# A gated MLP on one core: two plain hidden tiles in place of three, the norm's row left out of eight tiles and applied to their product sums later, sums split at full width

## The chip, the cores and the metric

The kernel runs on one core of a Trainium2 chip. The metric is device time in microseconds (us). The kernel before took 1174.26, 1174.37 and 1175.05 us in three runs, median 1174.37. Its profiled execution is a fourth one, of 1175.14 us.

The engines of a core run their own instruction streams side by side and wait for each other by semaphores: PE (matmuls), DVE (vector), ACT (scalar), POOL and SP. In this kernel SP issues the loads, POOL the stores that add to what is in DRAM.

## The reference, cut to what matters

The network has two layers over 512 positions of width 1024. Each layer ends in a gated MLP with 2816 hidden columns; `x` is float32.

```python
def rmsnorm(x, g):
    y = x * lax.rsqrt(jnp.mean(x * x, axis=-1, keepdims=True) + EPS)
    return y * g

def conv_ffn(h, w_up, conv_w, conv_b, w_down):
    u, g = jnp.split(h @ w_up, 2, axis=-1)
    g = causal_dwconv(g, conv_w, conv_b)      # width 3 over positions
    return (jax.nn.silu(g) * u) @ w_down

x = x + conv_ffn(rmsnorm(x, norm_ffn_g[l]), ffn_w_up[l], ffn_conv_w[l], ffn_conv_b[l], ffn_w_down[l])
```

The factor of the norm is one number for each position. It must be in the gate before the convolution and the silu; the other factor `u`, and everything behind it, is linear in it.

## The kernel before

Activations lie transposed: 128 features by 512 positions in a tile, so `x` has 8 tiles and the hidden layer 22. The norm's factors, one for each position and the same in all partitions, are a tile of 128x512, the row (`norm.row`). Every operand of a matmul is split into a high part (ACT: a cast, line 143) and a low part (DVE: source minus high, line 144), and `mm3` (lines 197 to 199) makes three matmuls of a product.

`ChannelMixer` is the MLP of one layer. Its input is scaled by `gain` alone: the row is multiplied into gate and up after the projection, so that the projections of the first tile need not wait for the norm. Hidden tiles come in two ways:

- **Plain tiles** (`plain(j)`, j below `PLAIN` = 3): gate and up, 8 products each, 48 matmuls of 512 columns. Then gate times row (line 773), the convolution's three taps (one on ACT, two on DVE in line 744), silu, times row (line 778), times up (line 781), and the split into the pair `hid[j]`. The finish of the norm is woven into the first plain tile: a sum of squares, a matmul with ones, and five short operations that make the row.
- **Block steps** (`step(j)`, j from 3 to 21): gate and up of a tile together in seven block products instead of eight. Each has 4 products of 256 columns, 84 matmuls in all. Their operands are sums and differences of weight blocks (DVE, line 944) and of blocks of the activations. The latter, `block_sums` (four pairs of tiles: 4 differences of 256 columns, line 799, then 4 splits of 256 for each pair), are needed from the first step on and are woven between the projections: `EARLY` and `BEHIND_NORM` say where, and `weave` puts one behind every 16 products. `Forms` loads and prepares the weights of one step ahead, `Tail` finishes the tile of one step behind (row on the gate in line 996, on up in line 999, taps, silu, product, split).

Behind the hidden tiles come the down products: `LOADS` lists pieces of the down weights, as hidden tiles k0 to k1 and output tiles j0 to j1; `UNITS` gives each step its pieces, one from step 3 on. `down_products` makes the matmuls for one output tile in a PSUM tile (`ptr`), `add` copies it to SBUF (ACT, line 825), and POOL adds it to `xspill` in DRAM (line 826), which holds `x`. The first two pieces take hidden tiles 0 and 1 for four output tiles each (24 matmuls of 512 columns), the next four tiles 2 and 3 for two output tiles (12 matmuls), the rest four hidden tiles for two output tiles (24). The last 6 hidden tiles are multiplied by the stage that follows, after `x` is read back.

In the block steps the order on PE, ACT and DVE is the order in which the code is written (`manual_schedule`); in the plain stage and on SP and POOL a scheduler sets it. All queues are worked off in order: what stands behind a waiting instruction waits too. Weight tiles of 128x1024 are loaded into three buffers (`wr`), so a load goes out when the third load before it has been split.

Of the kernel before, what the change touches and what calls it, by code (L numbers as in the profile page):

```python
# [39 lines left out]

PLAIN, LAST = 3, 6
LOADS = [(0, 2, 0, 4), (0, 2, 4, 8)]
LOADS += [(2, 4, 2 * i, 2 * i + 2) for i in range(4)]
LOADS += [(4 * g, 4 * g + 4, 2 * i, 2 * i + 2) for g in (1, 2, 3) for i in range(4)]
EARLY, BEHIND_NORM = ({4: 1, 5: 1}, {7: 1}), (1, 1)
UNITS = {3 + i: tuple((i, j) for j in range(*LOADS[i][2:])) for i in range(len(LOADS))}

H = S // 2  # L50

# [6 lines left out]
def trunk(  # L58
# [34 lines left out]
    def sb(tag, shape, dtype=F32):  # L93
        count[0] += 1
        return pool.tile(shape, dtype, tag=tag, name=f"{tag}{count[0]}", bufs=bufs[tag])
# [46 lines left out]
    def split(hi, lo, src, on_act=True, pinned=False):  # L142
        high = A.copy(hi, src) if on_act else V.tensor_copy(hi, src)  # L143
        low = V.tensor_tensor(out=lo, in0=src, in1=f(hi), op=ALU.subtract)  # L144
        if pinned:
            pin(high)
            pin(low)
# [575 lines left out]
    class ChannelMixer:  # L723
# [9 lines left out]
        def __init__(self, l, gain, beside):  # L733
            self.l, self.act, self.norm, self.gain, self.beside = l, [], Norm(), gain, beside
            self.forms = self.block_sums()
            self.w, self.fw, self.fb = ffn_w_up[l], col[f"fw{l}"], col[f"fb{l}"]
            self.hid, self.down, self.loaded = [], {}, set()


        def taps(self, j, acc, src):  # L740
# [19 lines left out]
        def plain(self, j):  # L760
            gate = project(self.w, DFF + j * P, self.act)
            up = project(self.w, j * P, self.act, "sc")
            if self.norm.row is None:
                both = pair_of(gate, up)
                weave(self.norm.finish(), both, 1)
                for _ in range(BEHIND_NORM[self.l]):
                    next(self.forms)
                og, ou = yield from both
            else:
                og = yield from gate  # L770
                ou = None
            acc, src = sb("t", [P, S]), sb("t", [P, S])
            V.tensor_tensor(out=src, in0=og, in1=self.norm.row, op=ALU.mult)
            self.last_tap(j, acc, src)
            for _ in self.taps(j, acc, src):
                pass
            A.activation(acc, acc, AF.Silu)
            V.tensor_mul(acc, acc, self.norm.row)
            if ou is None:
                ou = yield from up  # L780
            V.tensor_tensor(out=acc, in0=ou, in1=acc, op=ALU.mult)
            self.keep(acc)

        def block_sums(self):

            self.sums = []
            for k in range(KT // 2):
                b1, b2 = sb("u", [P, S]), sb("u", [P, S])
                for t, i in ((b1, k), (b2, k + KT // 2)):
                    A.activation(t, xT[i], AF.Copy, scale=self.gain[:, i : i + 1])  # L790
                forms = []
                ta, tb = sb("t", [P, S]), sb("t", [P, S])
                for o, x, y in (
                    (ta[:, :H], b1[:, H:], b1[:, :H]),
                    (ta[:, H:], b2[:, H:], ta[:, :H]),
                    (tb[:, :H], b2[:, H:], b1[:, H:]),
                    (tb[:, H:], b2[:, :H], ta[:, H:]),
                ):
                    V.tensor_tensor(out=o, in0=x, in1=y, op=ALU.subtract)
                for t in (ta, tb):  # L800
                    for h in (t[:, :H], t[:, H:]):
                        both = sb("u", [P, S], F32R)
                        split(both[:, :H], both[:, H:], h)
                        forms.append(both)
                self.sums.append(forms)
                yield

# [6 lines left out]
        def down_products(self, q, j):  # L814
            k0, k1, j0, _ = LOADS[q]
            w = self.down[q]
            o = ps("tr")
            c = slice((j - j0) * P, (j - j0 + 1) * P)
            for k in range(k0, k1):
                mm3(o, w[0][:, k - k0, c], w[1][:, k - k0, c], *self.hid[k], k == k0, k == k1 - 1)  # L820
            return j, o

        def add(self, j, o):
            t = sb(("bias", "t")[self.l], [P, S])
            A.copy(t, o)  # L825
            G.dma_start(xspill[j], t, accum_op=ALU.add)  # L826


# [19 lines left out]

        def t(self, i):

            return [(p[i - 1][:, :H], p[i - 1][:, H:]) for p in self.sums]

        def later(self):

# [22 lines left out]
        def step(self, j, w, nxt, tail):  # L877
            def then(o, *names):
                for name in names if o is not None else ():
                    getattr(o, name)()  # L880

            def sum_products(o, r, w, i):

                self.products(r, w, self.t(i))
                A.copy(o, r[:, :H])  # L885

            new = Tail(self, j)
            then(tail, "last_block", "scaled")
            w.split_fourth()
            then(tail, "scaled_up")  # L890
            r1, r2, new.r3 = ps("mm"), ps("mm"), ps("sc")
            new.up, new.u3, new.pre = sb("t", [P, S]), sb("t", [P, S]), sb("t", [P, S])
            self.products(r1, w.a11, self.b(0, 0), True)
            A.copy(new.up[:, :H], r1[:, :H])
            then(tail, "first_tap", "second_tap", "third_tap")
            self.products(r2, w.a12, self.b(1, 0), True)
            V.tensor_tensor(out=new.up[:, :H], in0=new.up[:, :H], in1=r2[:, :H], op=ALU.add)
            sum_products(new.up[:, H:], r1, w.s2, 2)
            then(tail, "silu")
            then(nxt, "sums")  # L900
            self.products(new.r3, w.s1, self.t(1), True)
            then(tail, "gated")
            then(nxt, "split_second", "sum_third")
            sum_products(new.u3[:, :H], r1, w.s3, 3)
            then(tail, "split")
            then(nxt, "split_up")
            V.tensor_tensor(out=new.pre[:, H:], in0=new.u3[:, :H], in1=new.r3[:, :H], op=ALU.add)
            w.down_products(0, 2)
            then(nxt, "split_sums", "sum_fourth")
            w.add_down(0)  # L910
            then(nxt, "split_gate")
            w.add_down(1)
            then(nxt, "split_down")
            sum_products(new.pre[:, :H], r1, w.a22, 4)
            w.down_products(2, 4)
            self.products(new.r3, w.s4, self.b(1, 1))
            w.add_down(2)
            w.add_down(3)
            return new, nxt

    class Forms:
# [63 lines left out]
    class Tail:  # L985
# [10 lines left out]
            V.tensor_mul(self.pre, self.pre, self.mixer.norm.row)  # L996

        def scaled_up(self):
            V.tensor_mul(self.up, self.up, self.mixer.norm.row)

        def first_tap(self):
            self.acc = sb("t", [P, S])
# [591 lines left out]
```

## Time and profile before

| what | value |
|---|---|
| median of three runs | 1174.37 us |
| profiled execution / its span | 1175.14 / 1173.4 us |
| granted clock of TensorE | 0.998 |
| ACT, POOL busy, share of the span | 63%, 12% |
| layer 0: plain tiles 0, 1, 2 | 273.76, 285.13, 296.01 to 306.89 us |
| layer 1: first plain tile from | 825.80 us |
| low parts of 128x1024 (line 144) | 172, mean 1138 ns |
| row on up (line 999) | 38, mean 686 ns |
| stores from line 826 | 80, layer 0 median 6.1 us to landing, layer 1 5.9 us |

Times in a row of a timeline are its start and its length in us. A matmul's row shows its whole length, which overlaps the next one: what it costs is the distance to the start of the next. The same holds for DVE, where an operation's last part overlaps the next one's start. Where a row has brackets at its end, the engine sat idle before it for so many us, and the arrow names what it waited for.

### The profile page before, as it was taken

What the parts mean: (1) busy time and instruction counts of PE and PEld (TensorE: products, weight loads), DVE (VectorE), ACT (ScalarE), POOL (GpSimd) and SP (SyncE); (2) the same over time, 40 slices, a digit from 0 to 9 for tenths busy, and PEclk for the clock granted to TensorE, in tenths of its full rate; (3) what the DMA queues carried; (4) which work ended last, traced back from release to release, by engine and by line L of the source; (5) the groups of instructions that cost most, each with busy time, mean ns of one, the idle gap of its engine ahead of it and who ended that gap; (6) DMA issues with size and microseconds to landing.
All of it is one profiled execution on the core that took longest, in us unless ns stands there. A gap on an engine that the chain in (4) does not pass through costs nothing.

```text
span 1173.4 us, 19109 instructions
## 1 busy us (share of the span) xinstructions
PE 1163.2 (99%) x7149; PEld 1035.1 (88%) x7149; DVE 983.8 (84%) x1768; ACT 744.2 (63%) x1345; POOL 143.0 (12%) x238
## 2 busy tenths in 40 slices
PE   9999999999999999999999999999999999999997
PEld 9988888888899999999888888778789999999986
DVE  6777788888999988888788888897999998888865
ACT  6548677657666655555676676776766765555545
POOL 1111101000031211111020000101011111110100
PEclk9999999999999999999999999999999999999999
DMA  8645325244478866665573313335447776666551
GB/s 288 221 110 139 89 55 153 77 140 133 108 176 194 199 168 167 145 143 119 153 215 108 90 55 104 97 91 179 142 100 161 154 147 143 142 144 144 126 161 73
DMA packets 200623, 162.87 MB, mean 139 GB/s; under 512 B 8680, under 2 KB 176334, under 8 KB 200530
## 3 DMA queue, kind: packets, MB, share of 16 engines
q1 hardware_dynamic: 182066, 119.74, 34.8%
q0 software_dynamic: 17888, 40.86, 18.2%
q8 instruction: 56, 0.92, 0.3%
q10 hardware_dynamic: 576, 1.05, 0.2%
q14 instruction: 37, 0.30, 0.1%
HBM read 128.89 MB, written 36.66 MB: 141 GB/s over the span
## 4 chain that ended last, share of the span: by engine, by line
PE 96%; DVE 2%; ACT 1%; DMA 0%; issue 0%; POOL 0%; POOLq 0%; DVEq 0%
PE pmm L197 19%; PE pmm L198 18%; PE pmm L199 18%; PE ptr L198 6%; PE ptr L197 6%; PE ptr L199 6%; PE psc L198 5%; PE psc L199 5%; PE psc L197 5%; PE psc L603 2%; PE ptr L1416 1%; PE ptr L1437 1%; PE ptr L1438 1%; PE ptr L672 1%; PE pmm L494 0%; PE ptr L686 0%
## 5 line engine op out<-in xcount | busy, mean ns | idle before, releaser
L197 PE MATMUL pmm<-u,wh 128*128 128x512 f32 (+1 forms) x984 | 334.2, 340 | 0.2 <-ACT u L143 0.2
L199 PE MATMUL pmm<-u,wl 128*128 128x512 f32 (+1 forms) x984 | 331.6, 337 | 0.0
L198 PE MATMUL pmm<-u,wh 128*128 128x512 f32 (+1 forms) x984 | 331.4, 337 | 0.0
L144 DVE TENSOR_TENSOR wl<-wr,wh 128x1024 fp32r<-128x1024 f32 (+4 forms) x172 | 195.8, 1138 | 74.9 <-ACT wh L143 74.2
L143 ACT CAST wh<-wr 128x1024 fp32r<-128x1024 f32 (+4 forms) x172 | 168.5, 982 | 78.8 <-PE pmm L198 30.8
L199 PEld LDWEIGHTS pmm<-u,wl 128*128 128x128 f32 x984 | 184.8, 188 | 19.5
L197 PEld LDWEIGHTS pmm<-u,wh 128*128 128x128 f32 x984 | 184.9, 188 | 17.3 <-ACT u L143 1.0
L198 PEld LDWEIGHTS pmm<-u,wh 128*128 128x128 f32 x984 | 185.0, 188 | 16.8 <-DVE u L144 0.5
L197 PE MATMUL ptr<-u,wh 128*128 128x512 f32 x272 | 106.6, 392 | 0.0
L198 PE MATMUL ptr<-u,wh 128*128 128x512 f32 x272 | 106.3, 391 | 0.0
L199 PE MATMUL ptr<-u,wl 128*128 128x512 f32 x272 | 105.8, 389 | 0.0
L143 ACT CAST fh<-pt 128x512 fp32r<-128x512 f32 x114 | 71.3, 626 | 34.4 <-DVE pt L944 33.6
L885 ACT COPY t<-pmm 128x256 f32<-128x256 f32 x114 | 42.5, 373 | 69.4 <-PE pmm L199 69.1
L197 PE MATMUL pmm<-u,fh 128*128 128x256 f32 x304 | 84.4, 278 | 0.0
L198 PE MATMUL pmm<-u,fh 128*128 128x256 f32 x304 | 84.1, 277 | 0.0
L199 PE MATMUL pmm<-u,fl 128*128 128x256 f32 x304 | 84.0, 276 | 0.0
L144 DVE TENSOR_TENSOR fl<-pt,fh 128x512 fp32r<-128x512 f32 x114 | 78.4, 688 | 4.3 <-ACT fh L143 1.4
L744 DVE SCALAR_TENSOR_TENSOR t<-t,cols,t 128x511 f32<-128x511 f32 x88 | 66.0, 750 | 8.8 <-ACT t L751 7.5
L197 PE MATMUL psc<-u,wh 128*128 128x256 f32 (+1 forms) x216 | 67.2, 311 | 0.0
L198 PE MATMUL psc<-u,wh 128*128 128x256 f32 (+1 forms) x216 | 67.0, 310 | 0.0
L199 PE MATMUL psc<-u,wl 128*128 128x256 f32 (+1 forms) x216 | 67.0, 310 | 0.0
L826 POOL DMA_DIRECT2D xspill<-t x40 | 34.2, 870 | 258.0 <-ACT t L825 244.8
(350 smaller groups left out, 2619.8 us busy)
## 6 DMA issues: line engine op xcount, KB each, us to landing
wr<-in_ffn_w_up_dram SPq DMA_DIRECT2D x50, 512.0 KB, 8.2
pt<-in_ffn_w_up_dram SPq DMA_DIRECT2D x38, 512.0 KB, 8.1
wr<-in_ffn_w_down_dram SPq DMA_DIRECT2D x34, 512.0 KB, 5.5
wr<-in_a_w_in_dram SPq DMA_DIRECT2D x20, 512.0 KB, 3.9
xspill<-bias POOLq DMA_DIRECT2D x40, 256.0 KB, 6.1
xspill<-t POOLq DMA_DIRECT2D x40, 256.0 KB, 5.9
wr<-in_w_kv_dram SPq DMA_DIRECT2D x12, 512.0 KB, 4.0
xspill<-fh POOLq DMA_DIRECT2D x16, 256.0 KB, 2.6
```

What stands on the lines that cost most here:

```text
L143: high = A.copy(hi, src) if on_act else V.tensor_copy(hi, src)
L144: low = V.tensor_tensor(out=lo, in0=src, in1=f(hi), op=ALU.subtract)
L197: nc.tensor.matmul(o, lh, rh, start=first, stop=False, skip_group_check=more)
L198: nc.tensor.matmul(o, lh, rl, start=False, stop=False, skip_group_check=more)
L199: nc.tensor.matmul(o, ll, rh, start=False, stop=last, skip_group_check=more)
L603: nc.tensor.matmul(o, a, b, start=first and i == 0, stop=i == 1)
L672: nc.tensor.transpose(tp[:, a, i, :], es[T2, h][:, i, a * P : (a + 1) * P], ident)
L744: V.scalar_tensor_tensor(acc[:, n:], src[:, : S - n], self.fw[:, c * FT + j : c * FT + j + 1], acc[:, n:], op0=ALU.mult, op1=ALU.add,)
L826: G.dma_start(xspill[j], t, accum_op=ALU.add)
L885: A.copy(o, r[:, :H])
L1416: nc.tensor.transpose(tp[:, b * P : (b + 1) * P], es[T, h][:, b * P : (b + 1) * P], ident)
L1437: nc.tensor.matmul(o2[:, s * P :], w, hi_at(pts[h], s, s, TT - s), start=s == 0, stop=False)
```

## The change

Four edits, the same in both layers:

1. `PLAIN` is 2: hidden tile 2 becomes a block step. Steps run from 2 to 21, and `UNITS` starts with step 2. The second piece of `LOADS` is cut in two, so that step 2 has four output tiles and steps 3 and 4 two each; the last piece stays with step 20.
2. For hidden tiles 0 to 7 (`LATE` = 8) the row is not multiplied into the second factor. Their down products are summed in a DRAM array of their own, `without_row` (`self.y`), one for each layer: the first pair is stored, the others are added. In steps 11 to 18 one output tile of it is loaded at the step's beginning (`load_late`, SP), multiplied by the row at its end (`late_row`, DVE) and added to `xspill` (POOL).
3. In the first step the first two down products stand ahead of the second sum product, in place of behind the fifth of the seven products.
4. `block_sums` splits whole tiles of 512 columns: 2 casts and 2 low parts for each pair of tiles where there were 4 and 4 of 256.

```diff
-PLAIN, LAST = 3, 6
-LOADS = [(0, 2, 0, 4), (0, 2, 4, 8)]
+PLAIN, LAST, LATE = 2, 6, 8
+LOADS = [(0, 2, 0, 4), (0, 2, 4, 6), (0, 2, 6, 8)]
...
-UNITS = {3 + i: tuple((i, j) for j in range(*LOADS[i][2:])) for i in range(len(LOADS))}
+LATE_ROW = {11: 2, 12: 3, 13: 4, 14: 5, 15: 0, 16: 1, 17: 6, 18: 7}
+UNITS = {PLAIN + i: tuple((i, j) for j in range(*LOADS[i][2:])) for i in range(len(LOADS))}
...
             A.activation(acc, acc, AF.Silu)
-            V.tensor_mul(acc, acc, self.norm.row)
             if ou is None:
...
                 for t in (ta, tb):
-                    for h in (t[:, :H], t[:, H:]):
-                        both = sb("u", [P, S], F32R)
-                        split(both[:, :H], both[:, H:], h)
-                        forms.append(both)
+                    hi, lo = sb("u", [P, S], F32R), sb("u", [P, S], F32R)
+                    split(hi, lo, t)
+                    forms += [(hi[:, :H], lo[:, :H]), (hi[:, H:], lo[:, H:])]
...
+        def add(self, q, j, o):
+            k0, k1, _, _ = LOADS[q]
             t = sb(("bias", "t")[self.l], [P, S])
             A.copy(t, o)
+            if k0:
+                G.dma_start((self.y if k1 <= LATE else xspill)[j], t, accum_op=ALU.add)
+            else:
+                G.dma_start(self.y[j], t)
+
+        def load_late(self, j):
+            t = sb("bias", [P, S])
+            nc.sync.dma_start(t, self.y[j])
+            return t
+
+        def late_row(self, j, t):
+            V.tensor_mul(t, t, self.norm.row)
             G.dma_start(xspill[j], t, accum_op=ALU.add)
...
             new = Tail(self, j)
+            late = self.load_late(LATE_ROW[j]) if j in LATE_ROW else None
...
             self.products(r2, w.a12, self.b(1, 0), True)
+            if j == PLAIN:
+                w.down_products(0, 2)
...
-            w.down_products(0, 2)
+            if j > PLAIN:
+                w.down_products(0, 2)
...
             w.add_down(3)
+            if late is not None:
+                self.late_row(LATE_ROW[j], late)
...
         def scaled_up(self):
-            V.tensor_mul(self.up, self.up, self.mixer.norm.row)
+            if self.j >= LATE:
+                V.tensor_mul(self.up, self.up, self.mixer.norm.row)
```

The lines of the changed kernel have higher numbers: `mm3` is 198 to 200, a low part 145, a block sum's difference 800, a weight sum 963.

Three places show how instructions move. First PE in layer 0, where the second block product of the first step ends (`pmm`, 256 columns; `u_2994`, in the new kernel `u_2987`, is the last activation). Before, with step 3 as the first, the second sum product follows:

```order
L197 MATMUL pmm_3330<-u_2994,wh_3291 128x256
L198 MATMUL pmm_3330<-u_2995,wh_3291 128x256
L199 MATMUL pmm_3330<-u_2994,wl_3292 128x256
L197 MATMUL pmm_3329<-u_2847,fh_3297 128x256
L198 MATMUL pmm_3329<-u_2847,fh_3297 128x256
```

Now, with step 2 as the first, the down products of hidden tiles 0 (`u_3096` high, `u_3097` low) and 1 (`u_3190`, `u_3191`) follow there:

```order
L198 MATMUL pmm_3238<-u_2987,wh_3199 128x256
L199 MATMUL pmm_3238<-u_2988,wh_3199 128x256
L200 MATMUL pmm_3238<-u_2987,wl_3200 128x256
L198 MATMUL ptr_3268<-u_3096,wh_3215 128x512
L199 MATMUL ptr_3268<-u_3097,wh_3215 128x512
L200 MATMUL ptr_3268<-u_3096,wl_3216 128x512
L198 MATMUL ptr_3268<-u_3190,wh_3215 128x512
L199 MATMUL ptr_3268<-u_3191,wh_3215 128x512
L200 MATMUL ptr_3268<-u_3190,wl_3216 128x512
```

The down products moved ahead of 36 matmuls of the sum products; the first that reads the low half of hidden tile 1 is the fifth of them.

Second, DVE in layer 0 around the sum of squares of the norm (`rb_2792`, now `rb_2793`: the last addition and its low part). Before:

```order
L144 TENSOR_TENSOR u_2915<-t_2901,u_2915 128x256
L333 SCALAR_TENSOR_TENSOR u_2955<-fl_2372,cols_449,u_2954 128x512
L716 TENSOR_TENSOR fl_2374<-fl_2374,pmm_2964 128x512
L144 TENSOR_TENSOR wl_3046<-wr_3043,wh_3045 128x1024
L292 TENSOR_TENSOR rb_2792<-rb_2792,t_2991 128x512
L333 SCALAR_TENSOR_TENSOR u_2995<-fl_2374,cols_449,u_2994 128x512
L144 TENSOR_TENSOR t_2999<-rb_2792,t_2998 128x512
L144 TENSOR_TENSOR wl_3117<-wr_3114,wh_3116 128x1024
```

Now:

```order
L145 TENSOR_TENSOR u_2908<-t_2898,u_2907 128x512
L963 TENSOR_TENSOR pt_3101<-pt_3101,wr_3195 128x512
L334 SCALAR_TENSOR_TENSOR u_2948<-fl_2372,cols_449,u_2947 128x512
L293 TENSOR_TENSOR rb_2793<-rb_2793,t_2984 128x512
L145 TENSOR_TENSOR wl_3200<-wr_3195,wh_3199 128x1024
L334 SCALAR_TENSOR_TENSOR u_2988<-fl_2374,cols_449,u_2987 128x512
L145 TENSOR_TENSOR t_2992<-rb_2793,t_2991 128x512
L145 TENSOR_TENSOR fl_3206<-pt_3101,fh_3205 128x512
L963 TENSOR_TENSOR pt_3101<-wr_3195,pt_3100 128x512
L963 TENSOR_TENSOR pt_3101<-wr_3195,pt_3101 128x512
```

The first step's operands (`wr_3195`, its up weights, and the differences in `pt_3101` of line 963, with their low parts) stand ahead of and among the norm's rows.

Third, DVE in layer 0 up to the low half of hidden tile 1. Before (`u_3109` is that of tile 0, `u_3208` that of tile 1):

```order
L778 TENSOR_TENSOR t_3145<-t_3145,rb_3060 128x512
L799 TENSOR_TENSOR t_3188<-u_3185,t_3188 128x256
L799 TENSOR_TENSOR t_3189<-u_3185,u_3184 128x256
L799 TENSOR_TENSOR t_3189<-u_3185,t_3188 128x256
L144 TENSOR_TENSOR u_3194<-t_3188,u_3194 128x256
L144 TENSOR_TENSOR u_3197<-t_3188,u_3197 128x256
L144 TENSOR_TENSOR u_3200<-t_3189,u_3200 128x256
L144 TENSOR_TENSOR u_3203<-t_3189,u_3203 128x256
L781 TENSOR_TENSOR t_3145<-psc_3159,t_3145 128x512
L773 TENSOR_TENSOR t_3243<-pmm_3217,rb_3060 128x512
L144 TENSOR_TENSOR fl_3298<-pt_3113,fh_3297 128x512
L144 TENSOR_TENSOR u_3208<-t_3145,u_3207 128x512
```

Now (`u_3191` is that of tile 1):

```order
L145 TENSOR_TENSOR u_3097<-t_3088,u_3096 128x512
L746 SCALAR_TENSOR_TENSOR t_3133<-t_3134,cols_799,t_3133 128x510
L800 TENSOR_TENSOR t_3175<-u_3171 128x256
L800 TENSOR_TENSOR t_3176<-u_3172,u_3171 128x256
L800 TENSOR_TENSOR t_3175<-u_3172,t_3175 128x256
L145 TENSOR_TENSOR wl_3216<-wr_3197,wh_3215 128x1024
L800 TENSOR_TENSOR t_3176<-u_3172,t_3175 128x256
L145 TENSOR_TENSOR u_3182<-t_3175,u_3181 128x512
L782 TENSOR_TENSOR t_3133<-psc_3146,t_3133 128x512
L145 TENSOR_TENSOR u_3186<-t_3176,u_3185 128x512
L913 TENSOR_TENSOR t_3240<-t_3240,pmm_3238 128x256
L145 TENSOR_TENSOR u_3191<-t_3133,u_3190 128x512
```

Between the two hidden tiles' low halves the last block sums and the low part of the down weights (`wl_3216`) stand now; the multiplication by the row (line 778) is gone, and no gate of a third plain tile is there.

More of the change, by code (lines that the diff above doesn't have):

```diff
@@ L737, in __init__ @@
             self.hid, self.down, self.loaded = [], {}, set()
+            self.y = dram.tile([KT, P, S], F32, name=f"without_row{l}")
         def taps(self, j, acc, src):
@@ L820, in down_products @@
                 mm3(o, w[0][:, k - k0, c], w[1][:, k - k0, c], *self.hid[k], k == k0, k == k1 - 1)
-            return j, o
-        def add(self, j, o):
+            return q, j, o
+        def add(self, q, j, o):
+            k0, k1, _, _ = LOADS[q]
             t = sb(("bias", "t")[self.l], [P, S])
             A.copy(t, o)
+            if k0:
[8 more added lines that the diff above has]
+            V.tensor_mul(t, t, self.norm.row)
             G.dma_start(xspill[j], t, accum_op=ALU.add)
@@ L849, in t @@
         def t(self, i):
-            return [(p[i - 1][:, :H], p[i - 1][:, H:]) for p in self.sums]
+            return [p[i - 1] for p in self.sums]
         def later(self):
```

## The prediction

> **What bounds the kernel now.** I read the page first: busy shares, then the chain that ended last.
>
> ```profile
> PE 1163.2 (99%) x7149; PEld 1035.1 (88%) x7149; DVE 983.8 (84%) x1768; ACT 744.2 (63%) x1345; POOL 143.0 (12%) x238
> ...
> PE 96%; DVE 2%; ACT 1%; DMA 0%; issue 0%; POOL 0%; POOLq 0%; DVEq 0%
> ```
>
> TensorE (PE) is busy for 99% of the span, and 96% of the chain is matmuls. So a matmul that goes is worth its length, provided that its operands come in time, and DVE at 84% is the engine that could fail to bring them. The share is a mean over stages, so I cut both mixers into stretches (columns: length, then busy time and count of PE, weight loads, DVE, ACT, POOL; granted clock; DMA share; GB/s).
>
> ```profile
> 273.76:285.13 11.37, 11.37 (x51) 9.39 (x50) 9.60 (x17) 7.62 (x14) 1.65 (x3) 1.00 0.61 167
> 285.13:296.01 10.88, 10.88 (x49) 9.01 (x48) 9.07 (x15) 8.09 (x12) 0.00 (x0) 1.00 0.21 55
> 296.01:306.89 10.88, 10.88 (x50) 9.01 (x48) 10.88 (x21) 6.42 (x11) 0.00 (x0) 1.00 0.29 92
> ...
> 338.74:387.79 49.05, 49.05 (x386) 47.09 (x385) 47.85 (x74) 34.16 (x60) 12.76 (x18) 1.00 0.85 188
> 430.00:505.00 75.00, 75.00 (x543) 70.22 (x542) 65.00 (x95) 43.98 (x76) 12.26 (x17) 1.00 0.63 152
> ...
> 825.80:836.70 10.90, 10.14 (x45) 8.10 (x44) 9.04 (x17) 9.62 (x17) 0.54 (x1) 1.00 0.41 128
> ...
> 847.60:862.00 14.40, 14.40 (x75) 12.26 (x74) 14.40 (x28) 11.60 (x21) 0.00 (x0) 1.00 0.36 109
> ```
>
> The first three rows are layer 0's plain tiles 0, 1 and 2. The third, the tile that becomes a block step, has DVE busy for all of its 10.88 us. The fourth row is four steps of the short kind (12 down matmuls), 12.26 us each; the fifth is five of the long kind (24 down matmuls), 15.0 us each, with DVE at 13.0. The last row is layer 1's third plain tile and what follows: DVE full again. **The plain stage is where DVE has nothing to spare.**
>
> **The tile itself.** A plain tile is 48 matmuls of 512 columns, 10.88 us (second row). A block step is 84 of 256 besides its down products. The down products are as many as before, and 12 of them cost 12 x 10.88/48 = 2.72 us, so a step's own products cost 12.26 - 2.72 = 9.54 us. Gain: 10.88 - 9.54 = 1.34 us for each layer, **-2.68 us** in all, if PE never waits.
>
> **What DVE has to do before the first block step.** Unit prices are the distances between starts of neighbouring rows.
>
> ```profile
> 267.29 1.44 DVE L144 TENSOR_TENSOR u<-t,u 128x256 fp32r<-128x256 f32 x4
> ...
> 280.54 1.22 DVE L144 TENSOR_TENSOR wl<-wr,wh 128x1024 fp32r<-128x1024 f32 x1 [1.67 <-ACT wh L143]
> 281.68 0.68 DVE L305 TENSOR_SCALAR rb<-psc 128x512 f32<-128x512 f32 x1
> 282.28 0.42 DVE L799 TENSOR_TENSOR t<-u 128x256 f32<-128x256 f32 x1
> 282.61 0.69 DVE L309 SCALAR_TENSOR_TENSOR t<-t,rb 128x512 f32<-128x512 f32 x1
> ...
> 290.77 0.69 DVE L773 TENSOR_TENSOR t<-pmm,rb 128x512 f32<-128x512 f32 x1 [1.34 <-PE pmm L199]
> ...
> 843.22 0.74 DVE L744 SCALAR_TENSOR_TENSOR t<-t,cols,t 128x510 f32<-128x510 f32 x1
> 843.88 0.68 DVE L773 TENSOR_TENSOR t<-pmm,rb 128x512 f32<-128x512 f32 x1
> ```
>
> So 0.60 us for 512 columns (281.68 to 282.28), 0.33 for 256, 0.66 for the conv's row (843.22 to 843.88), 1.14 for the 1024-wide low part (280.54 to 281.68). The wider split replaces two of 256, 0.67 together, by one of 512 at 0.60: 8 x 0.07 = 0.5 us less DVE in each layer (it is in the counts below). The norm's multiplication that leaves each plain tile is 0.60.
>
> Against that stands what moves forward. The first step's low parts, differences and sums were spread over three plain tiles and now must fit beside two. In layer 0 the order is the same in both kernels up to the row at 267.29, which is then a 512-wide split. From there to the low half of hidden tile 1, which the second pair of down products reads, the changed order has 55 DVE rows: 7 of 1024, 7 of the conv's form, 13 of 256, 28 of 512. That is 7 x 1.14 + 7 x 0.66 + 13 x 0.335 + 28 x 0.60 = 33.8 us, done at 267.29 + 33.8 = 301.1. The two gaps above (1.67 for a cast, 1.34 for plain tile 1's gate) are filled by the rows that moved there, so I count no gap for them.
>
> When is it due? PE gets to the first step at 296.01, where plain tile 2 stood.
>
> ```profile
> 306.66 0.39 PE L199 MATMUL psc<-u,wl 128*128 128x512 f32 x1
> 306.89 0.28 PE L197 MATMUL pmm<-u,wh 128*128 128x256 f32 x1
> 307.01 0.28 PE L198 MATMUL pmm<-u,wh 128*128 128x256 f32 x1
> ```
>
> The first 24 block matmuls take 24 x 0.1137 (9.54/84) = 2.73 us. Then, because the down products are moved ahead of the second sum, come four matmuls that read hidden tile 0 and the high half of tile 1 (0.91 us), and the fifth reads the low half: due at 296.01 + 3.64 = 299.65. It stands at the head of PE's queue: the other 19 down matmuls and all the products after them wait behind it, though the operands of several of them are ready. In the old place, after the fifth of the seven products instead of the second, the same matmul would have been due 36 x 0.1137 = 4.1 us later. **New wait: 301.1 - 299.65 = 1.45 us, as the least.**
>
> One term is uncertain. Ahead of the norm's last square now stands a difference that reads the first step's up weights. Their transfer goes out when the buffer of the up weights of plain tile 0 is free, which is when DVE has made their low part: 272.0 by the same sum. The difference's turn is at 275.8. From issue to landing:
>
> ```profile
> wr<-in_ffn_w_up_dram SPq DMA_DIRECT2D x7, 512.0 KB, 3.9
> ...
> wr<-in_ffn_w_up_dram SPq DMA_DIRECT2D x3, 512.0 KB, 5.1
> ```
>
> The upper row is the median from 255 to 300 us, the lower that of the three issued from 267 to 285. Landing is then at 275.9 to 277.1, so DVE waits 0.1 to 1.3 us; I take 0.7, the middle, since the two rows are equally near. Layer 0: a wait of **2.2 us** (1.5 to 3.0), net 2.2 - 1.34 = **+0.85**.
>
> **Layer 1** has the same shape, but waits already.
>
> ```profile
> 826.00 0.69 DVE L716 TENSOR_TENSOR fl<-fl,pmm 128x512 f32<-128x512 f32 x1 [0.76 <-PE pmm L199]
> 827.38 0.69 DVE L292 TENSOR_TENSOR rb<-rb,t 128x512 f32<-128x512 f32 x1 [0.70 <-ACT t L291]
> ...
> 834.32 1.23 DVE L144 TENSOR_TENSOR wl<-wr,wh 128x1024 fp32r<-128x1024 f32 x1 [0.79 <-ACT wh L143]
> ```
> ```profile
> 831.01 0.39 PE L199 MATMUL pmm<-u,wl 128*128 128x512 f32 x1
> 832.15 0.50 PE L302 MATMUL psc<-t,onesr 128*128 128x512 f32 x1 [0.76 <-ACT t L143]
> 832.49 0.39 PE L197 MATMUL psc<-u,wh 128*128 128x512 f32 x1
> ```
> ```profile
> 862.83 0.37 PE pmm L197
> ...
> 871.51 0.50 PE ptr L197
> ```
>
> PE starts the norm's matmul 1.14 us after its predecessor where 0.23 is usual: 0.91 us lost. The last two rows are pieces of the chain, where a 256-column matmul takes 0.114 and a 512-column one 0.227: 0.26 + 0.27 = 0.53 lost in the old first step. From the row at 826.00 to tile 1's low half the changed order has 46 DVE rows: 5 x 1.14 + 5 x 0.66 + 12 x 0.335 + 24 x 0.60 = 27.4, so 853.4 without gaps. Both gaps above (0.70, 0.79) may stay, and the transfer of the up weights (buffer free about 825.3, due about 829.0) is as tight as in layer 0. ACT, which ends such gaps, is busy 9.62 of the 10.90 us. I take 1.5. PE is due at 825.80 + 2 x 10.88 + 0.68 for the norm's two matmuls + 3.64 = 851.9. Wait: 853.4 + 1.5 + 0.1 - 851.9 = **3.1 us** (1.6 to 4.3). The norm's cast stands earlier in the new order, so of its 0.91 I keep 0.2; the 0.53 goes with the old first step. Net: -1.34 + 3.1 + 0.2 - 0.91 - 0.53 = **+0.5**.
>
> **After the first step** DVE catches up during the wait, and each step with a tail below tile 8 loses a multiplication of 0.60, where the short steps had 47.85 of 49.05 busy. I count no wait there; without that cover it would show as idle time of PE in steps 3 to 8. **The late rows** add one multiplication of 0.69 to each of eight long steps, where DVE has 75.0 - 65.0 = 10 us free in five, 2.0 each: nothing. Each brings a load and an accumulating store of 256 KB.
>
> ```profile
> 426.89 0.92 POOL L826 DMA_DIRECT2D xspill<-bias  x1 [3.15 <-ACT bias L825]
> ...
> 428.52 0.37 SPq L156 DMA_DIRECT2D wr<-in_ffn_w_down_dram  x1
> 429.06 0.58 SPq L836 DMA_DIRECT2D pt<-in_ffn_w_up_dram  x1
> 431.54 0.37 SPq L156 DMA_DIRECT2D wr<-in_ffn_w_up_dram  x1
> ...
> 450.70 0.69 DVE L944 TENSOR_TENSOR pt<-pt 128x512 f32<-128x512 f32 x1
> ...
> xspill<-bias POOLq DMA_DIRECT2D x40, 256.0 KB, 6.1
> ...
> DMA to landing us min/median/max: 3.8/8.1/11.1
> ```
>
> The tightest is the first: row tile 2 is complete when the store at 426.89 has landed, 6.1 us later: 433.0. Until then SP stands at its load, with the next gate and up weights (429.06, 431.54) queued behind. Put off to 433.6, the gate lands by 444.7 at the worst (11.1, the last row, of these gate loads), and is first read at 450.70. The late load itself has from 433.0 to the end of the step, about 443. POOL's added store waits for the multiplication at the step's end; behind it stands the next step's first store, due more than 10 us into that step (426.89 in a step that began at 413). Bounds: nothing, or 0.69 for each of 16 late rows if DVE's cover is gone; I take nothing.
>
> **Sum:** +0.85 + 0.5, with the roundings **+1.4 us**. The profiled execution took 1175.14 us around its span of 1173.4, 0.8 above the median of 1174.37; on that execution 1176.5, on the median **1175.8 us**. The lower bounds (1.45 and 1.6 for the waits) give -0.9, the upper (3.0 and 4.3, with the old 0.53 kept) about +3.9: 1173.5 to 1178.3.
>
> **Rivals.**
>
> 1. *PE stays covered.* Then only the saving counts, and in layer 1 the old waits may go too: -2.68 to -4.1, 1171.7 to 1170.3. For it: the third row of the windows has no PE wait although DVE is full. Against: 33.8 us of DVE work stand from 267.29 to a matmul due 32.4 us later, with no gap left to fill. Chance 0.20.
> 2. *The weights' transfer decides (slower).* The difference at DVE's head waits for the up weights, behind it the norm's square, its matmul, the row, and through the row both hidden tiles. Each us of landing over 3.9 is then a us of PE, in both layers. By the 8.1 us of the gate loads of the steps: 4.2 - 0.7 = 3.5 more in one layer, or some 1.8 in each: about 1179. It decides from a landing of 5.1. For it: the lower of the two transfer rows; against: DMA share is 0.61 and less in this stage. Chance 0.20.
> 3. *The wait slows what follows (slower).* If PE, after a wait of 3.1 us, ran at half pace for as long again, that is 1.55 us more in layer 1: 1177.4. The trace speaks against it for short waits: after the 0.91 us the matmuls stand 0.23 apart and the clock is 1.00. Chance 0.05. The Trainium skill ("TensorE: Matmul & The Clock Gate", Part 1) says that PE's clock falls to half after an idle window of about 3.4 us, and is restored after such a window of work; by it the forecast wait is just too short, the upper bound not, and no run here shows it.
> 4. *The change does not keep its late rows hidden:* 16 x 0.69 = 11 us at the most, 1187, if the load comes last in each step. Against: the slack above. Chance 0.03.
>
> **How the numbers follow.** The forecast has the remaining 0.52, its own range 1173.5 to 1178.3, about 0.09 of it above 1176.7. A measurement tells 0.2% (2.35 us) from no change: faster is below 1172.0 (rival 1, and no part of the forecast), 0.20; slower 0.20 + 0.05 + 0.03 + 0.09, less the part of rivals 2 and 3 that ends below 1176.7 (0.05), 0.32; the same 0.48. The range leaves out half of rival 1 and the far ends of 2 and 4: 1170.9 to 1179.2.
>
> **What would show it.** In the profile after: PE idle 1.5 to 3 us before a down product (ptr) that waits for DVE's low part of a hidden tile near 300 us, and 1.6 to 4.3 near 852; no such wait afterwards; nothing near the late multiplications. If DVE stands idle for a transfer near 276 us, rival 2 is at work; no wait at ptr, rival 1; distances of 0.45 between matmuls behind the wait, rival 3. The forecast is wrong if DVE's rows are shorter than here, if its work was not what plain tile 2 gave cover to, or if the catching up reaches into steps 3 and 4.

## The result, and the profile after

The changed kernel takes 1181.8 us (median of 5, 1179.44 to 1183.29) against 1174.63 us before (median of 5): ratio 1.0058, 95% interval 1.0042 to 1.0074. It is slower by some 7 us, five times what I had forecast and outside the range. The profiled execution is the longest of the five, 1183.29 us.

The page's lines on busy time and the chain:

```profile
PE 1165.0 (99%) x7221; PEld 1038.3 (88%) x7221; DVE 991.1 (84%) x1774; ACT 747.2 (63%) x1345; POOL 151.1 (13%) x254
...
PE 27%; DVE 2%; ACT 1%; issue 0%
```

They hide what happened: PE is "99% busy" again. Its idle time grew from 10.2 us (1173.4 - 1163.2) to 15.3 (1180.3 - 1165.0), which a share of some 1180 us does not show. Its busy time, which should have lost 2.7 us, grew by 1.8: a matmul at a lower clock counts as busy for longer. (The chain could be followed back over 30% of the span only.) The list of PE's waits says more, in us, with the number of times and the longest:

```profile
PE ptr L198 <- ACT u L144: 2.2, 2, 1.1
...
PE ptr L199 <- DVE u L145: 1.0, 2, 0.7
PE pmm L198 <- ACT t L898: 0.9, 2, 0.5
PE ptr L198 <- ACT bias L826: 0.7, 1, 0.7
PE ptr L198 <- ACT t L826: 0.7, 1, 0.7
```

The first two lines are the forecast wait, for the high and the low half of hidden tile 1, once in each layer. The other three are waits that the prediction does not have. PE's timeline in layer 0 shows where:

```profile
299.16 0.39 PE L200 MATMUL ptr<-u,wl 128*128 128x512 f32 x1
300.64 0.50 PE L198 MATMUL ptr<-u,wh 128*128 128x512 f32 x1 [1.09 <-ACT u L144]
301.52 0.50 PE L199 MATMUL ptr<-u,wh 128*128 128x512 f32 x1 [0.38 <-DVE u L145]
301.86 0.40 PE L200 MATMUL ptr<-u,wl 128*128 128x512 f32 x1
302.10 0.43 PE L198 MATMUL ptr<-u,wh 128*128 128x512 f32 x1
302.34 0.62 PE L199 MATMUL ptr<-u,wh 128*128 128x512 f32 x1
302.76 0.63 PE L200 MATMUL ptr<-u,wl 128*128 128x512 f32 x1
...
306.44 0.28 PE L198 MATMUL psc<-u,wh 128*128 128x256 f32 x1
...
309.05 0.28 PE L200 MATMUL pmm<-u,wl 128*128 128x256 f32 x1
309.79 0.38 PE L198 MATMUL pmm<-u,fh 128*128 128x256 f32 x1 [0.46 <-ACT t L898]
...
311.20 0.28 PE L200 MATMUL pmm<-u,fl 128*128 128x256 f32 x1
312.17 0.50 PE L198 MATMUL ptr<-u,wh 128*128 128x512 f32 x1 [0.69 <-ACT bias L826]
```

Distances between starts tell the cost. From 299.16 to 302.10 stand four matmuls that need 0.91 us and take 2.94: **2.0 us** of waiting for hidden tile 1. From 302.34 on the 512-column matmuls stand 0.42 apart in place of 0.23. Then two more gaps: 0.74 - 0.11 = 0.62 us ahead of the sixth block product, and 0.97 - 0.11 = 0.86 us ahead of the third down product. ACT's rows show what these two wait for:

```profile
309.36 0.37 ACT L898 COPY t<-pmm 128x256 f32<-128x256 f32 x1 [1.83 <-PE pmm L200]
309.63 1.05 ACT L144 CAST wh<-wr 128x1024 fp32r<-128x1024 f32 x1
310.58 1.05 ACT L144 CAST wh<-pt 128x1024 fp32r<-128x1024 f32 x1
311.52 0.59 ACT L826 COPY bias<-ptr 128x512 f32<-128x512 f32 x1
```

The first row copies the fifth product out of its PSUM tile (the accumulator in which matmuls add up), and the sixth adds into that tile. The last row copies the first down sum, behind two wide casts in ACT's queue, though that sum's last matmul had begun at 301.86; the third down product waits for its tile, and starts when the copy is over. The windows by the microsecond (the number behind POOL's is the granted clock) show what the wide distances are:

```profile
299.00:300.00 1.00, 0.55 (x3) 0.11 (x1) 1.00 (x3) 0.42 (x2) 0.00 (x0) 1.00 0.32 75
300.00:301.00 1.00, 0.36 (x1) 0.19 (x1) 1.00 (x3) 0.58 (x1) 0.00 (x0) 1.00 1.07 322
301.00:302.00 1.00, 0.62 (x3) 0.43 (x3) 1.00 (x2) 0.00 (x0) 0.00 (x0) 1.00 0.43 128
302.00:303.00 1.00, 1.00 (x5) 0.81 (x4) 0.76 (x2) 0.00 (x0) 0.00 (x0) 0.66 0.06 16
303.00:304.00 1.00, 1.00 (x3) 0.75 (x3) 0.00 (x0) 0.00 (x0) 0.00 (x0) 0.50 0.03 8
304.00:305.00 1.00, 1.00 (x5) 0.86 (x4) 0.00 (x0) 0.00 (x0) 0.00 (x0) 0.50 0.00 0
305.00:306.00 1.00, 1.00 (x8) 1.00 (x8) 0.00 (x0) 0.00 (x0) 0.00 (x0) 0.63 0.00 0
306.00:307.00 1.00, 1.00 (x11) 1.00 (x10) 0.00 (x0) 0.36 (x2) 0.00 (x0) 1.00 0.00 0
```

The clock is 1.00 through the wait and falls to half right behind it, for about 3.4 us; the 18 matmuls from 302.10 to 306.44 (six of 512 columns, twelve of 256) take 4.34 us in place of 2.72: **1.6 us**. DVE was full up to 302, as forecast, and then has nothing to do: it waits for PE.

So layer 0 loses 2.0 + 1.6 + 0.62 + 0.86 = 5.1 us and gains 1.34; step 5, measured from a matmul at 246 us that both kernels have, begins 4.0 us later than before. Layer 1 has the same four pieces (2.3 us from 855.32 to 858.52, then 1.6, 0.62 and 0.85), and the old waits of 0.92 and 0.33 (0.53 with the wider distance behind each, as the prediction counts it) are gone; its step 5 is 2.8 us later than before, measured in the same way from 614 us. From step 5 to the last step nothing differs: four short steps take 49.10 us (49.05 before), five long ones 75.0.

```profile
342.49:391.59 49.10, 49.10 (x386) 47.14 (x385) 46.62 (x72) 33.96 (x61) 11.70 (x16) 1.00 0.83 178
433.00:508.00 75.00, 75.00 (x543) 70.21 (x542) 66.94 (x100) 44.01 (x77) 15.29 (x19) 1.00 0.79 185
```

DVE has 46.62 us of work in the short steps where it had 47.85, and 66.94 in the long ones where it had 65.00: the late rows are there, and cost nothing.

### The profile page after: what moved, and what is told of

It is laid out like the page before. It is cut to its first block, busy times and chain, and to the rows that moved or that the text cites. A ratio compares the mean times of both kernels' runs of the same rounds, so it can differ in the third digit from the quotient of the medians.

```text
span 1180.3 us, 19333 instructions
## 1 busy us (share of the span) xinstructions
PE 1165.0 (99%) x7221; PEld 1038.3 (88%) x7221; DVE 991.1 (84%) x1774; ACT 747.2 (63%) x1345; POOL 151.1 (13%) x254
## 5 line engine op out<-in xcount | busy, mean ns | idle before, releaser
L198 PE MATMUL pmm<-u,wh 128*128 128x256 f32 (+1 forms) x992 | 334.6, 338 | 0.2 <-ACT u L144 0.2
L200 PE MATMUL pmm<-u,wl 128*128 128x256 f32 (+1 forms) x992 | 332.0, 335 | 0.0
L199 PE MATMUL pmm<-u,wh 128*128 128x256 f32 (+1 forms) x992 | 331.8, 334 | 0.0
L144 ACT CAST wh<-wr 128x1024 fp32r<-128x1024 f32 (+4 forms) x172 | 166.9, 972 | 76.3 <-PE pmm L199 33.8
L144 ACT CAST fh<-pt 128x512 fp32r<-128x512 f32 x120 | 74.9, 624 | 34.8 <-DVE pt L963 32.7
L145 DVE TENSOR_TENSOR fl<-pt,fh 128x512 fp32r<-128x512 f32 x120 | 82.3, 686 | 9.7 <-ACT fh L144 6.6
L198 PE MATMUL pmm<-u,fh 128*128 128x256 f32 x320 | 89.5, 280 | 0.9 <-ACT t L898 0.9
L199 PE MATMUL pmm<-u,fh 128*128 128x256 f32 x320 | 89.1, 278 | 0.0
L200 PE MATMUL pmm<-u,fl 128*128 128x256 f32 x320 | 88.9, 278 | 0.0
L198 PEld LDWEIGHTS ptr<-u,wh 128*128 128x128 f32 x272 | 51.3, 189 | 14.4 <-ACT u L144 3.0
L198 PEld LDWEIGHTS pmm<-u,fh 128*128 128x128 f32 x320 | 60.8, 190 | 3.6 <-ACT t L898 2.0
L198 PE MATMUL psc<-u,wh 128*128 128x256 f32 (+1 forms) x208 | 63.2, 304 | 0.0
L200 PE MATMUL psc<-u,wl 128*128 128x256 f32 (+1 forms) x208 | 62.9, 303 | 0.0
```

The costliest lines, as they stand in the source:

```text
L198: nc.tensor.matmul(o, lh, rh, start=first, stop=False, skip_group_check=more)
L199: nc.tensor.matmul(o, lh, rl, start=False, stop=False, skip_group_check=more)
L200: nc.tensor.matmul(o, ll, rh, start=False, stop=last, skip_group_check=more)
```

## The experiments

Every ratio is to the kernel before, run on the same chip; that kernel's median was 1175.16 us beside the first four runs, 1175.02 beside the next four, 1175.27 beside the last three.

### One edit undone, or one alone

**The place of the down products undone.** In step 2 they go back behind the fifth block product:

```diff
             self.products(r2, w.a12, self.b(1, 0), True)
-            if j == PLAIN:
-                w.down_products(0, 2)
...
-            if j > PLAIN:
-                w.down_products(0, 2)
+            w.down_products(0, 2)
```

> The changed kernel, but in step 2 the first two down products stand where they stand in every other step, behind the fifth of the seven block products. Theory A (the place of the down products makes all the waits): the matmul that reads hidden tile 1 is due 4.1 us later, after its operand; the third and the seventh block product, which share a PSUM tile, are apart again. No wait of PE at ptr, none of 0.6 and 0.9 us behind it, granted clock 1.00 throughout. Time: 1174.6 - 2.68 (the saved matmuls) - 1.25 (waits of before in layer 1 of 0.92 and 0.33 us) = 1170.7, at the most 1172. Rival B (DVE is behind by its load, wherever the products stand): PE waits about 2 us in each layer at the second sum or at the down products: 1175 to 1179.

Measured: 1178.37 us, ratio 1.0027 (1.0016 to 1.0037). By its time the run lies in rival B's range, but not with B's waits of 2 us in each layer. Theory A came out for layer 0: there all the waits of step 2 are gone, with the fall of the clock and both gaps behind it, and step 5 starts 1.06 us earlier than before (1.34 saved, 0.3 lost at the norm). In layer 1 there is a wait at the second sum, where rival B had put one, but longer. The waits of PE and ACT's timeline:

```profile
PE pmm L198 <- ACT t L908: 3.3, 1, 3.3
...
PE pmm L199 <- DVE u L145: 0.5, 1, 0.5
```
```profile
851.28 0.62 ACT L144 CAST u<-t 128x512 fp32r<-128x512 f32 x1 [0.59 <-DVE t L782]
851.81 0.72 ACT L791 ACTIVATE u<-fh,cols 128x512 f32<-128x512 f32 x1
852.43 0.71 ACT L791 ACTIVATE u<-fl,cols 128x512 f32<-128x512 f32 x1
853.04 0.35 ACT L908 COPY t<-pmm 128x256 f32<-128x256 f32 x1
```

The second sum adds into the PSUM tile of the first product, so it must wait until ACT has copied that (L908). The second sum was due at 850.0. But in ACT's queue the copy stands behind the cast of hidden tile 1, which waits for DVE (L782), and behind the inputs of the last block sum. So DVE's backlog of layer 1 reaches PE through ACT: 3.4 us, and a stretch at half clock behind it.

**The copies forward, the new place kept.** In step 2 the copies of the first two down sums stand right behind the fifth block product, and the sixth adds to the PSUM tile of the second product, not to that of the fifth; with that its sum is not the layer's. (The expectations call this product, `sum_products(new.pre[:, :H], r1, w.a22, 4)`, the seventh; in the code it is the sixth, and the seventh goes to another tile.)

```diff
             sum_products(new.u3[:, :H], r1, w.s3, 3)
+            if j == PLAIN:
+                w.add_down(0)
+                w.add_down(1)
...
-            w.add_down(0)
+            if j > PLAIN:
+                w.add_down(0)
...
-            w.add_down(1)
+            if j > PLAIN:
+                w.add_down(1)
...
-            sum_products(new.pre[:, :H], r1, w.a22, 4)
+            sum_products(new.pre[:, :H], r2 if j == PLAIN else r1, w.a22, 4)
```

> The changed kernel with the down products in their new place; in step 2 the copies of the first two down sums stand right behind the fifth block product on ACT, and the seventh block product takes the PSUM tile of the second in place of that of the fifth. Theory A: the waits of 0.62 and 0.86 us that follow the first wait in both layers come from PSUM tiles that are not read out in time; they go, 2 x 1.48 = 3.0 us, the first wait and the slow stretch of PE behind it stay: 1176.5 where the clock does not fall, 1179 to 1180 where it falls in both layers. Rival B (they are what is left of the DVE backlog): no change, 1179.5 to 1183.

Measured: 1178.57 us, ratio 1.0031 (1.0019 to 1.0042). The waits of PE:

```profile
PE ptr L198 <- ACT u L144: 2.2, 2, 1.1
PE pmm L474 <- DVE mcf L131: 1.1, 1, 1.1
PE ptr L199 <- DVE u L145: 1.0, 2, 0.7
PE ptr L480 <- DMA u<-in_mem_dram: 0.3, 1, 0.3
```

The first wait stands as it was, 2.2 and 1.0 us for both layers; the three lines on copies are gone. Theory A holds: the kernel is 3.4 us above before where the changed one is 7.2 above, 3.8 less; 3.0 were expected from the waits, and its runs have a mean clock of 0.997 or 0.999, where the changed kernel's go down to 0.995. The gaps of 0.62 and 0.86 us are not DVE's backlog, they come from what the down products left behind. Before, they stood between the fifth and the sixth block product, which use the same PSUM tile, and gave ACT time to copy it. And their two sums fill both `ptr` tiles long before ACT's queue comes to their copies, while the third waits for such a tile.

**The late rows alone**, on the kernel before with three plain tiles:

> The kernel before, with the late row alone: the row left out of hidden tiles 0 to 7, the second array, the loads, multiplications and stores of steps 11 to 18; three plain tiles and the splits as before. Theory A (late rows are hidden, and DVE is not the bound with three plain tiles): 1174.3, between 1173.6 and 1174.8. Rival C (what the second array moves costs time, inside the span or at its ends, where the changed kernel's time stands 2.0 to 3.0 us above its span and that of before 1.7): 1175.5 or more.

Measured: 1174.89 us, ratio 0.9998 (0.9989 to 1.0007). Theory A, by the ratio: five long steps from 430 us on have the late multiplications and take 75.0 us, with DVE busy for 66.99 of them.

**The wider splits alone** on the kernel before, `block_sums` as in the change:

> The kernel before, with the wider splits of the block sums alone. Theory A (0.5 us less of DVE in each layer, where PE does not wait): 1174.4, between 1173.6 and 1174.8, the wait at layer 1's norm 0.92 us or less. Rival D (the wide operands are read slower by PE, since the halves of a 512-wide tile lie apart): the 256-column matmuls of the sums stand more than 0.114 us apart, 1176 or more.

Measured: 1174.21 us, ratio 0.9992 (0.9983 to 1.0001); if anything a small gain. In its trace layer 1's norm costs PE 0.18 us in place of 0.92, and the 256-column matmuls of the sums stand 0.113 us apart as before, so rival D is out.

### What the times of one kernel differ by

> The changed kernel as it is, for more runs and another profile. Theory A (its runs differ by how often the granted clock falls to half behind the wait: in no layer, one or both): times in three groups about 1.7 us apart, each with its mean clock: about 1179.5 at 0.999, 1181.5 at 0.997, 1183 at 0.995; in the profile the waits at ptr are 1.1 and 0.4 us in each layer whatever the clock. Rival E (the waits themselves differ from run to run): times without groups, not tied to the clock.

Measured: 1181.94 us, ratio 1.0057 (1.0044 to 1.0069). Over both series, ten runs of the changed kernel by mean clock: 1179.4 and 1179.7 us at 0.999; 1180.3, 1180.9 and 1181.9 at 0.998; 1181.8, 1182.6 and 1183.1 at 0.997; 1182.9 and 1183.3 at 0.995. The order is that of theory A, the clear groups are not. The new profile decides it. PE's timeline at the same place of layer 0:

```profile
299.90 0.39 PE L200 MATMUL ptr<-u,wl 128*128 128x512 f32 x1
301.38 0.49 PE L198 MATMUL ptr<-u,wh 128*128 128x512 f32 x1 [1.09 <-ACT u L144]
302.26 0.50 PE L199 MATMUL ptr<-u,wh 128*128 128x512 f32 x1 [0.39 <-DVE u L145]
302.61 0.40 PE L200 MATMUL ptr<-u,wl 128*128 128x512 f32 x1
302.85 0.40 PE L198 MATMUL ptr<-u,wh 128*128 128x512 f32 x1
303.08 0.40 PE L199 MATMUL ptr<-u,wh 128*128 128x512 f32 x1
```

The same waits, 1.09 and 0.39 us, and behind them matmuls 0.23 apart: here the clock did not fall in layer 0. In layer 1 of the same run it fell to 0.50. The waits are the same in both profiles; whether the clock falls behind them differs.

### Layer 1's backlog

The next kernels have the down products in the old place. In the changed kernel layer 0 makes two of its four block sums ahead of the plain stage, layer 1 one, behind the eighth output tile of the stage before (`EARLY`, which counts from 0). First, layer 1 makes a second one, behind the sixth:

```diff
-EARLY, BEHIND_NORM = ({4: 1, 5: 1}, {7: 1}), (1, 1)
+EARLY, BEHIND_NORM = ({4: 1, 5: 1}, {5: 1, 7: 1}), (1, 1)
```

> The run with the down products in their old place, and besides layer 1 makes one of its four block sums two output tiles earlier, ahead of the plain stage, as layer 0 makes two; so all block sums stand ahead of hidden tile 1 on DVE, and on ACT the copy of the first block product stands ahead of the cast of hidden tile 1. Theory A (layer 1's wait of 3.4 us is DVE's backlog of about 2.5 us, one block sum, with the copy queued behind it on ACT): PE waits under 1 us in step 2 of layer 1, the clock stays at 1.00; against 1175.2 of before on the chip of the last runs 1175.2 - 2.68 - 1.25 + 0.5 = 1171.8, between 1170.5 and 1173. Rival B (DVE has too much to do from 810 us on, whatever comes first): a wait of 2 us or more in layer 1 at another place, a drop of the clock, 1175 to 1178.

Measured: 1174.75 us, ratio 0.9999 (0.9990 to 1.0007). Layer 1's wait falls from 3.4 to 0.97 (still ACT's copy) and 0.88 us (the sums), the clock stays at 1.00 behind them in the profile, and the kernel is 3.5 us faster than with the old place alone, each against before on its own chip. Theory A in its cause, not in its size: the time is 3 us above the forecast. Of that, 1.85 us of waits remain where 0.5 was allowed, layer 0's norm costs PE 0.4, which was not counted, and 0.4 comes outside the span (device time less the profiled span, 2.1 us here and 1.7 before); 0.8 stays open.

With `{4: 1, 5: 1}` in layer 1 too:

> The same, but layer 1 makes two of its block sums ahead of the plain stage, behind the fifth and the sixth output tile, as layer 0 does. Theory A: as the last or a little faster, 1170.5 to 1172.5. Rival B: the norm's sum of squares comes later on DVE by 2.5 us, and PE waits for the norm's row near 832 us by 1 us or more: 1172.5 to 1175.

Measured: 1174.03 us, ratio 0.9991 (0.9982 to 1.0000). Step 2 has no wait over 0.3 us left, but rival B is right about the price, in another place: 1.7 us near 820 us, where PE waits for the low part of the output weights, behind a block sum on DVE.

```profile
PE pmm L200 <- DVE wl L145: 1.5, 1, 1.5
```

**Without the late row**, else as the first kernel of this part:

> The first kernel of this set without the late row: every hidden tile is multiplied by the row as in the kernel before, no second array, no loads, multiplications and stores of steps 11 to 18. Theory A (the late row gives DVE the 1.2 us in the plain stage and the 0.6 us in each of steps 3 to 8 that two plain tiles need): PE waits 1 us or more in each layer's step 2 or 3, 1173.5 to 1177. Rival F (with the old place DVE has room enough): within 0.7 us of the first kernel of this set.

Measured: 1179.06 us, ratio 1.0036 (1.0023 to 1.0048). That is 4.3 us more than with it: PE waits 0.57, 0.38 and 0.88 us in layer 0's step 2, 0.96, 0.66 and 1.42 in layer 1's, and behind those of layer 1 the clock falls. So theory A's waits came, and the time lies above its range. What differs ahead of them are two multiplications of 0.60 us in each plain stage. No wait shows in the short steps 3 to 8, so that half of theory A is not needed.

**Half of the products moved.** The six matmuls of the first two down products that read hidden tile 0 alone go ahead of the second sum (`first_products` takes hidden tile 0, k = 0 of both), the other six stay (`second_products`, k = 1):

```diff
             self.products(r2, w.a12, self.b(1, 0), True)
+            if j == PLAIN:
+                w.first_products(0, 2)
...
-            w.down_products(0, 2)
+            if j == PLAIN:
+                w.second_products(0, 2)
+            else:
+                w.down_products(0, 2)
```

> The kernel with the old place and one block sum of layer 1 earlier (behind the sixth and the eighth output tile); besides, in step 2 the half of the first two down products that reads hidden tile 0 alone (6 matmuls, 1.36 us) stands ahead of the second sum product, the half that reads hidden tile 1 stays in the old place. Theory A (PE waits 0.97 and 0.88 us in layer 1's step 2 because the copy and the sums come 1 to 2 us late, and hidden tile 0 is there long before): the waits of 1.85 us in layer 1 shrink by 1.36, none in layer 0: 1.4 us below that kernel, ratio to before 0.9985 to 0.999. Rival G (the copy of the first block product waits in ACT's queue for DVE, and work put before it changes nothing for DVE): 1174.8, ratio 1.000.

Measured: 1174.94 us, ratio 0.9995 (0.9986 to 1.0004). The waits of 0.97 and 0.88 shrink to 0.43, but a wait of 1.1 us for the copies of the down sums appears behind the sixth product, ahead of the third down product, and 0.26 of the same in layer 0. Neither theory had that. I read it as in the change itself, six matmuls missing at the old place; it was not tried apart.

> The same with layer 1's early block sums behind the sixth and the seventh output tile. Theory A: all sums stand ahead of the down weights and of hidden tile 1 on DVE, no wait in step 2 of either layer; ratio to before 0.9975 to 0.9985 (-2.68 - 1.25 of waits of before + 0.4 in layer 0's norm + 0.3 outside the span = -3.2 us at the best). Rival H (a block sum ahead of low parts of the output weights makes PE wait near 820 us as with sums behind the fifth and sixth): 1 us or more lost there, ratio 0.9985 to 1.

Measured: 1175.91 us, ratio 1.0006 (0.9997 to 1.0015). Neither: PE waits 1.9 us (2.1 by the distance of starts) for the low part of the down weights, which DVE now makes last, and behind that wait the clock falls in the profiled run.

> The same with layer 1's early block sums behind the seventh and the eighth output tile. Theory A: no wait near 820 us, in step 2 of layer 1 up to 1 us, since the last block sum ends behind the down weights: ratio 0.998 to 0.999. Rival H: a wait at the norm's matmul near 833 us of 0.9 us as before, ratio 0.9985 to 1.

Measured: 1174.07 us, ratio 0.9992 (0.9983 to 1.0001). Theory A in its waits: some 0.3, 0.8 and 0.5 us in layer 1's step 2, no other new wait; the ratio lies a little above its range. With the kernel of 1174.03 us it is the best found: 8 us below the changed kernel, level with the kernel before within the measurement.

## Why the prediction was wrong

**The matmuls saved: right.** Where no wait stood in the way (layer 0 with the old place) step 5 came 1.06 us earlier, 1.34 less the 0.3 lost at the norm.

**The forecast wait: right in place and cause, near in size.** 2.2 us were forecast in layer 0 and 2.0 came; 3.1 in layer 1 and 2.3 came. DVE's rows from the start of the sum to the low half of hidden tile 1:

```profile
267.01 0.68 DVE L145 TENSOR_TENSOR u<-t,u 128x512 fp32r<-128x512 f32 x1
...
275.77 0.69 DVE L963 TENSOR_TENSOR pt<-pt,wr 128x512 f32<-128x512 f32 x1 [0.20 <-DMA wr<-in_ffn_w_up_dram]
...
300.78 0.68 DVE L145 TENSOR_TENSOR u<-t,u 128x512 fp32r<-128x512 f32 x1
301.38 0.68 DVE L963 TENSOR_TENSOR pt<-pt 128x512 f32<-128x512 f32 x1
```

From 267.01 (267.29 in the kernel before) to 301.38 are 34.4 us, where 33.8 of rows and 0.7 for the transfer had given 34.5. That it fits so well is in part luck: the transfer of the up weights made DVE wait for 0.20 us, and the 55 rows took 0.4 longer than their sum. PE already stood at the fourth down matmul, for the high half that ACT makes, not at the fifth; both halves are made of one row of DVE, the product with up. (The 1.14 us for a 1024-wide low part in the sum is a distance between starts. The 1138 ns in the table of the kernel before is near it by chance: a mean over 172 low parts, of which 135 are 1024 wide, at 1224 ns each.) In layer 1 I kept gaps on DVE that went.

**The step that failed: the moved down products were costed by when they are due, and by nothing else.** I wrote that all the products after them "wait behind it", asked what the products find at their new place, and set down nothing for anything else; I did not ask what their old place had been covering. It was the time in which ACT copies the fifth product's PSUM tile, and that in which both `ptr` tiles are emptied. The sixth product and the third down sum come into that gap: 0.62 + 0.86 us in each layer, 3.0 us in all, which the run with the copies forward took away again. "After the first step" was too late to look for new waits: they came within it.

**The second step that failed: rival 3 got a chance of 0.05 and one layer.** Its price, 1.55 us, is near the 1.6 measured, by luck: it was half of the forecast wait of 3.1 us, while the stretch at half clock was 3.4 us long behind waits of 2.0 and 2.3 us alike. The sign that I named for it, matmuls 0.45 us apart, stands in the profile with 0.42. But the profiled run paid it in both layers, for waits shorter than the one for which I had set it down as unlikely. The evidence that I held against it, matmuls 0.23 apart behind a wait of 0.91 us, was about a shorter wait. The Trainium skill ("TensorE: Matmul & The Clock Gate", Part 1) speaks of a half clock after an idle window of about 3.4 us; I used that as a threshold. The trace differs: in the 3 us from 299 to 302 PE was busy for 0.55 + 0.36 + 0.62 = 1.5 us, no single wait was over 1.1 us, and the clock fell all the same.

The sum by these steps, for the profiled run: layer 0 -1.34 + 2.0 + 1.6 + 1.5 = 3.8 of 4.0 measured; layer 1 -1.34 - 0.92 - 0.33 + 2.3 + 1.6 + 1.5 + 0.25 (a wait at the norm) = 3.1 of 2.8. Without the fall of the clock it is 3.2 us less, 1180.1; the profiled run also has 3.0 us outside its span where the fastest have 2.1 and 2.2, which leaves 1179.2, near their 1179.4 and 1179.7.

**The rest.** The late rows are free in steps 11 to 18, as forecast, and they carry more than I gave them: without them two plain tiles cost 4.3 us more. Rival 1 (PE stays covered) is what layer 0 does with the old place. Rivals 2 and 4 did not happen.

## What to carry to other kernels

When work is moved, cost both places: the one where it may now wait, and the one that it leaves, where it may have covered a copy out of a PSUM tile or the turn of a buffer. A wait of PE of two microseconds, even in pieces, can cost nearly as much again in clock behind it, so cost it at its length and at its length plus that. And where an engine is full (DVE in the plain stage), the order of its last rows decides which other engine's queue carries the delay to PE: here ACT's, whose copy stood behind a cast that waited for DVE.

## What the runs showed of the hardware

- Behind some waits of PE the granted clock fell to half for 3.4 us. In layer 0 of the changed kernel, behind 2.0 us in two pieces, it fell in one profile and stayed at 1.00 in the other, and with the copies forward it stayed too; in layer 1, behind 2.3 us in two pieces, it fell in all three. It also fell behind a single wait of 2.1 us (block sums behind the sixth and the seventh tile), behind 3.0 us in three pieces (without the late row) and behind 3.4 us (the old place, where all eight runs have a mean clock of 0.996 or 0.997). It stayed at 1.00 in the profiles behind a single 1.7 us, behind 1.8 us in three pieces (without the late row, layer 0) and behind 0.97 and 0.88 us, 2.3 us apart.
- The kernels with two plain tiles take 2.0 to 3.3 us outside the span (without the late row 1.7 to 2.8), those with three plain tiles 1.7, the late row alone and the wider splits alone among them. In the median run that is 0.3 us of the result, in the profiled one 1.3; its cause is open, and no run tried it.
